# Two plain pairs of gate tiles, combinations in four steps, and scattered small loads in a two-layer encoder

## The chip, the cores and the metric

The kernel runs on one core of one Trainium2 chip. The metric is device time in microseconds (us) of one execution. The kernel before takes 3044.78 us (median of three runs, 3042.04 to 3044.88).

A core has a matrix engine (TensorE, PE in the profile), three engines for elementwise work (VectorE or DVE, ScalarE or ACT, GpSimd or POOL), and SyncE (SP), which here only starts transfers. TensorE reads its operands from on-chip memory and adds up in PSUM buffers, which another engine must empty. Each engine works through its own list of instructions in a fixed order; an instruction waits on semaphores for what others make, and what stands behind it on its engine waits with it. Transfers are started from SyncE's and GpSimd's lists.

## The reference

Two layers on 512 tokens of width 1024, in float32. Each layer is

```
h = h + 1/2 * SwiGLU_1(RMSNorm(h))
u = RMSNorm(h);  proj = u @ W_in
h = h + (sig(g_A)*o_A + sig(g_B)*o_B + sig(g_C)*o_C) @ W_out
h = h + 1/2 * SwiGLU_2(RMSNorm(h))
h = h + sigmoid(RMSNorm(h) @ W_pg) * (p[i] @ W_pp)
```

and the output is RMSNorm(h). A feed-forward is `(silu(x @ w_gate) * (x @ w_up)) @ w_down` with an inner width of 2816, that is 22 tiles of 128 ("gate tiles"; each has a gate and an up part). o_A is attention with low-rank queries and keys, o_B attention in a window of 128 with a logit for a sink, o_C the difference of two softmaxes, scaled by a learned lambda: `lam = exp(sum(lq1*lk1)) - exp(sum(lq2*lk2)) + lambda_init`. o_B and o_C add a bias that depends on the distance of two tokens and is looked up in a table of 32 buckets for 24 heads.

## The kernel before, in words

Every float32 value that TensorE uses is split in a high and a low part (`split` for activations, `Weights.part` for weights: a cast on ScalarE, names `whi`, `...h`, and a subtraction on VectorE or GpSimd, names `wlo`, `...l`). A product is then three matmuls (`mm3`): high by high, high by low, low by high. The activations stand transposed, 1024 features in 8 tiles of 128 x 512 tokens (`h`, in the trace `x`, `wo0h`, `wo1h`).

**A feed-forward** (`ffn`; ffn10 and ffn20 in layer 0, ffn11 and ffn21 in layer 1) works on the 22 gate tiles in 11 pairs. The first pair is *plain* (`plain_pair`): for each of its tiles f, 8 features by 3 matmuls of 512 columns for gate and as many for up. The norm's factor `rb` is multiplied in afterwards, so the matmuls can begin with the raw, gain-scaled `z` (`prep.z`). The other ten pairs are `Quad`s: the product of a 2 x 2 block of weights with a 2 x 2 block of activations (features in halves, tokens in halves A and B) is made with seven products instead of eight, each of 4 x 3 matmuls of 256 columns. The weights' sums are made by transfers that add (`accum_op`) and by `took`; the activations' combinations are made once for each feed-forward by `Combos.combine(k)` for k = 0 to 3: `t57k` for products 5 and 7, `t64k` for 6 and 4. The products of a pair come in the order 1, 2, then product 4 of the pair before, then 5, 6, 3, 7, each for gate (g) and up (u); V and R are the PSUM buffers of the results. So the first product that needs a combination is product 5 of the first `Quad`, after 48 matmuls of it. `gate_half` applies Silu and the norm factor (a multiply on GpSimd), `up_half` multiplies and splits to `a[f]`.

`DOWN_AFTER` says after which pair the down projection of a group of finished `a[f]` stands: group 0 (two tiles, 48 matmuls of 512 columns) after pair 1, group 1 (four tiles, 96 matmuls) after pair 3, and so on. Each of its eight results is added to `h[d]` by VectorE (L536).

**Order.** The code is written as one list of steps, with weight loads and splits prepared a fixed number of steps ahead (`load_upto`, `prepare`, `Weights`); a tile framework then places each engine's instructions by their dependencies and its own estimate of when they can run, so that instructions that wait for nothing late can move ahead of where the code has them. Whole weight chunks (512 KB) go through a ring of four buffers (`wraw`).

**Hooks** are small jobs that a feed-forward calls at a tile number f. In layer 0's first feed-forward: `load_tables` (f = 2, the bias table), `constants` (f = 4: the permutation matrix and, for each layer, the load of the four lambda vectors, two products, an exponential on ScalarE and the rest on VectorE), `bias_vectors` (f = 8: the table's lookups by matmul, their results `bvs` copied out and written to `bias_s` and `bias_d`, and then 24 transfers that spread each head's bias over 128 rows in `copies_s` and `copies_d`). The lambda loads and the bias copies are on GpSimd's queue.

Of the kernel before, what the change touches and what calls it, by code (L numbers as in the profile page):

```python
# [39 lines left out]
FFN_CHUNKS = 66  # L40

PAIRS = FT // 2
DOWN_AFTER = {1: 0, 3: 1, 5: 2, 7: 3}


def ffn_stream():

    res = []
    for p in range(PAIRS):
        res += [p] * 4  # L50
        if p in DOWN_AFTER:
            res += [None] * (2 if DOWN_AFTER[p] == 0 else 4)
    return res + [None] * 8


def whole(n):

    m = n % CHUNKS_PER_LAYER
    start = 0 if m < FFN_CHUNKS else CHUNKS_PER_LAYER - KT - FFN_CHUNKS
    return start <= m < start + FFN_CHUNKS and bool(ffn_stream()[m - start])  # L60


def lambda_init(i):
# [113 lines left out]
def encoder_kernel(ctx: ExitStack, tc: tile.TileContext, ins, out):  # L177
# [95 lines left out]
        return small[:, l * S_N + at:l * S_N + at + 1]  # L273

    def constants():
        nc.gpsimd.dma_start(perm, ins["perm"])
        for l in range(L):
            s = slice(l * NH, (l + 1) * NH)
            nc.vector.tensor_scalar(neg_sink[:, s], small[:, l * S_N + S_SINK:l * S_N + S_SINK + NH], -1.0, None, op0=ALU.mult)
            nc.vector.tensor_scalar(sub_gain[:, l:l + 1], col(l, S_SUB), 1.0 - lambda_init(l), None, op0=ALU.mult)  # L280
            lv = S(f"lamv{l}")
            nc.gpsimd.dma_start(lv[:, 0:256], ins["lam"][l])
            e = tiny(f"lam{l}")
            for j in range(2):
                pr = S(f"lamp{l}{j}")
                nc.vector.tensor_mul(pr[:, 0:64], lv[:, j * 128:j * 128 + 64], lv[:, j * 128 + 64:j * 128 + 128])
                nc.vector.tensor_reduce(e[:, j:j + 1], pr[:, 0:64], axis=AX.X, op=ALU.add)
            nc.scalar.activation(e[:, 2:4], e[:, 0:2], AF.Exp)

            nc.vector.tensor_scalar(e[:, 4:5], e[:, 3:4], -lambda_init(l), None, op0=ALU.add)  # L290
            nc.vector.tensor_sub(neg_lam[:, l:l + 1], e[:, 4:5], e[:, 2:3])
    tab, oh = [], []

    def load_tables():
        tab.append(S("tab"))
        nc.gpsimd.memset(tab[0][32:33, 0:24], 1.0)
        nc.gpsimd.dma_start(tab[0][0:32, 0:24], ins["rel_table"])
        for i in range(3):
            oh.append(S(f"oh{i}"))
            nc.gpsimd.dma_start(oh[i][0:33, :], ins["onehot"][:, i * 512:(i + 1) * 512])  # L300

    def bias_vectors():

        for i in range(3):
            ps = PS(f"bv{i}")
            heads = slice(0, NH) if i == 0 else slice(NH, NH + NHD)
            n = heads.stop - heads.start
            nc.tensor.matmul(ps[0:n, :], tab[0][0:33, heads], oh[i][0:33, :], start=True, stop=True)
            bv = S(f"bvs{i}")
            nc.vector.tensor_copy(bv[0:n, :], ps[0:n, :])  # L310
            if i == 0:
                nc.gpsimd.dma_start(bias_s, bv[0:n, :])
            else:
                nc.gpsimd.dma_start(bias_d[:, (i - 1) * 512:i * 512], bv[0:n, :])
        for vec, copies in ((bias_s, copies_s), (bias_d, copies_d)):
            for i in range(vec.shape[0]):
                nc.gpsimd.dma_start(copies[i], vec[i:i + 1, :].to_broadcast([P, vec.shape[1]]))

    def strip(vec, row, cols, tag, bufs, name, pool=sb):

# [188 lines left out]
    def ffn(l, tag, prep, after, hooks={}):  # L509
# [27 lines left out]
                if final:  # L537
                    after(d)

        def plain_pair():  # L540

            for f in range(2):
                pg, pu = PS(f"{name}g{f}"), PS(f"{name}u{f}")
                gate, up = ("cols", tag + "_w_gate", l, f), ("cols", tag + "_w_up", l, f)
                if f == 0:
                    together((pg, pu), W.get(gate, up), prep.z)
                    rstd()
                    prep.quarters()
                else:
                    run(proj(pg, W.get(gate), prep.z))  # L550
                    run(proj(pu, W.get(up), prep.z))
                g1, u1 = S(f"{name}g1_{f}"), S(f"{name}u1_{f}")
                nc.vector.tensor_mul(g1, pg, rb[0])
                nc.scalar.activation(g1, g1, AF.Silu)
                nc.vector.tensor_mul(u1, pu, rb[0])
                nc.vector.tensor_mul(u1, u1, g1)
                a[f] = split(u1, f"{name}a{f}")
                for k in (2 * f, 2 * f + 1):
                    prep.combine(k)

        def gate_half(q, n):

# [22 lines left out]
            steps.append(("product", (q, i), do))  # L585

        tail = []
        for p in range(1, PAIRS):
            G, U = [Quad(f"{name}{x}{p}", tag + "_w_" + w, p, prep) for x, w in (("g", "gate"), ("u", "up"))]
            for i in (1, 2):  # L590
                product(G, i)
# [14 lines left out]
            steps.insert(at + 2 + k, steps.pop())  # L606
        down(len(GROUPS) - 1, True)

        plain_pair()


        quads = []
# [33 lines left out]
        def prepare():  # L646
# [3 lines left out]
            load_upto(n + LOADS)  # L650
            if kind == "down":
                place = base[what]
                W.load(place + 1)
                hi, lo = W.tiles(stage)
                W.part(hi, lo, W.raw.pop(place))
                ready[n] = (hi, lo), state["tiles"]
                state["tiles"] += 1
                W.split = max(W.split, place + 1)
# [633 lines left out]
    for l in range(L):  # L1292
# [4 lines left out]
            18: lambda: p2.__setitem__(slice(0, 2), [split(t, f"p{l}_{k}") for k, t in enumerate(p2)]),  # L1297
        }
        if l == 0:
            hooks.update({2: load_tables, 4: constants, 8: bias_vectors})  # L1300
        ffn(l, "ffn1", prep, pm, hooks)
        close_stage()
        sums, outs = mix(l, pm, p2)
# [186 lines left out]
```

## Time and profile before

| | |
|---|---|
| median of 3 runs | 3044.78 us (3042.04 to 3044.88) |
| the profiled execution | 3043.61 us, span 3041.8 us |
| TensorE, VectorE, ScalarE, GpSimd busy | 96%, 71%, 55%, 37% of the span |
| mean granted clock of TensorE | 0.986 |
| matmuls in the trace | 17086 |

The view of waits reads "engine, what it was about to do, <- whom it waited for: us in total, times, longest". A row of the timeline or the chain begins with the start in us from the span's start, then the duration in us. The windows' table gives for a stretch the busy time of each engine with its instructions, the granted clock, the share of the DMA engines and GB/s. A group's row ends with the count, busy time and mean duration in ns, and the idle time before it with what ended most of it.

### The profile page before, as it was taken

What the parts mean: (1) busy time and instruction counts of PE and PEld (TensorE: products, weight loads), DVE (VectorE), ACT (ScalarE), POOL (GpSimd) and SP (SyncE); (2) the same over time, 40 slices, a digit from 0 to 9 for tenths busy, and PEclk for the clock granted to TensorE, in tenths of its full rate; (3) what the DMA queues carried; (4) which work ended last, traced back from release to release, by engine and by line L of the source; (5) the groups of instructions that cost most, each with busy time, mean ns of one, the idle gap of its engine ahead of it and who ended that gap; (6) DMA issues with size and microseconds to landing.
All of it is one profiled execution on the core that took longest, in us unless ns stands there. A gap on an engine that the chain in (4) does not pass through costs nothing.

```text
span 3041.8 us, 45943 instructions
## 1 busy us (share of the span) xinstructions
PE 2930.9 (96%) x17086; PEld 2566.1 (84%) x17086; DVE 2158.9 (71%) x3580; ACT 1666.8 (55%) x3201; POOL 1114.2 (37%) x1033
## 2 busy tenths in 40 slices
PE   7989999999999998999989999999999999899997
PEld 5879977888888888999879998788888878799996
DVE  7756767645788768777677777766467877676676
ACT  5434446655677755444454444566566777544453
POOL 2243213443445552333222331144444455432313
PEclk8999999999999999999989999999999999999999
DMA  6576342112222253656425553311212122655532
GB/s 209 145 226 165 95 161 70 56 63 76 80 72 69 77 185 98 172 154 165 140 70 160 146 153 128 117 63 56 70 68 81 62 79 82 191 142 142 151 96 83
DMA packets 116127, 351.21 MB, mean 115 GB/s; under 512 B 14222, under 2 KB 16270, under 8 KB 115904
## 3 DMA queue, kind: packets, MB, share of 16 engines
q1 hardware_dynamic: 78480, 261.39, 25.5%
q0 software_dynamic: 35120, 83.95, 12.6%
q8 instruction: 134, 2.20, 0.3%
q10 hardware_dynamic: 2304, 2.94, 0.3%
q14 instruction: 89, 0.73, 0.1%
HBM read 337.68 MB, written 18.94 MB: 117 GB/s over the span
## 4 chain that ended last, share of the span: by engine, by line
PE 76%; DVE 11%; ACT 5%; issue 4%; DMA 3%; POOL 1%; ACTq 0%; DVEq 0%; SPq 0%; POOLq 0%
PE ffn21d L218 4%; PE ffn11d L218 4%; PE ffn10d L218 4%; PE ffn20d L218 4%; PE ple L218 3%; DVE wlo L101 2%; PE m0ga L218 1%; PE m1ga L218 1%; PE m0gb L218 1%; PE m1gb L218 1%; PE m0vc L218 1%; PE m1vc L218 1%; PE m0qc L218 1%; PE m0kc L218 1%; PE m1qb L218 1%
## 5 line engine op out<-in xcount | busy, mean ns | idle before, releaser
L101 POOL TENSOR_TENSOR wlo<-wraw,whi 128x1024 fp32r<-128x1024 f32 x144 | 349.1, 2427 | 385.6 <-ACT whi L100 342.7
L100 ACT CAST whi<-wraw 128x1024 fp32r<-128x1024 f32 x296 | 310.5, 1051 | 212.5 <-issue 60.4
L101 DVE TENSOR_TENSOR wlo<-wraw,whi 128x1024 fp32r<-128x1024 f32 x152 | 189.9, 1252 | 93.3 <-ACT whi L100 92.9
L536 DVE SCALAR_TENSOR_TENSOR wo0h<-ffn11d,wo0h 128x512 f32<-128x512 f32 x48 | 32.9, 688 | 31.1 <-PE ffn11d L218 31.1
L536 DVE SCALAR_TENSOR_TENSOR wo1h<-ffn21d,wo1h 128x512 f32<-128x512 f32 x48 | 32.9, 688 | 29.2 <-PE ffn21d L218 29.2
L536 DVE SCALAR_TENSOR_TENSOR wo0h<-ffn20d,wo0h 128x512 f32<-128x512 f32 x48 | 32.9, 688 | 28.4 <-PE ffn20d L218 28.4
L536 DVE SCALAR_TENSOR_TENSOR x<-ffn10d,x 128x512 f32<-128x512 f32 x48 | 32.7, 687 | 25.4 <-PE ffn10d L218 25.4
L351 POOL TENSOR_TENSOR f_1sq<-f_1sq,f_1sq 128x512 f32<-128x512 f32 x14 | 21.5, 1533 | 42.9 <-ACT f_1sq L346 42.7
L894 ACT CAST m0kc<-m0kc 64x512 fp32r<-64x512 f32 x32 | 18.6, 582 | 18.5 <-PE m0kc L218 15.2
L894 ACT CAST m1kc<-m1kc 64x512 fp32r<-64x512 f32 x32 | 18.6, 582 | 18.5 <-PE m1kc L218 15.2
L847 DVE SCALAR_TENSOR_TENSOR m1qc<-m1qc,m1qc 64x512 fp32r<-64x512 f32 x16 | 11.0, 688 | 20.0 <-ACT m1qc L846 19.9
L847 DVE SCALAR_TENSOR_TENSOR m0qc<-m0qc,m0qc 64x512 fp32r<-64x512 f32 x16 | 11.0, 688 | 20.0 <-ACT m0qc L846 19.9
L846 ACT ACTIVATE m1qc<-m1qc 64x512 fp32r<-64x512 f32 x16 | 9.5, 594 | 21.4 <-PE m1qc L218 13.2
L846 ACT ACTIVATE m0qc<-m0qc 64x512 fp32r<-64x512 f32 x16 | 9.5, 593 | 21.4 <-PE m0qc L218 13.2
L1141 ACT ACT_TABLE_LOAD x16 | 20.5, 1283 | 0.3
L1313 POOL TENSOR_SCALAR out<-wo1h,small 128x512 f32<-128x512 f32 (+1 forms) x9 | 7.2, 795 | 33.0 <-DVE wo1h L1277 33.0
L351 POOL TENSOR_TENSOR pg0sq<-pg0sq,pg0sq 128x512 f32<-128x512 f32 x7 | 10.6, 1513 | 23.1 <-ACT pg0sq L346 23.1
L351 POOL TENSOR_TENSOR pg1sq<-pg1sq,pg1sq 128x512 f32<-128x512 f32 x7 | 10.6, 1512 | 23.1 <-ACT pg1sq L346 23.1
L915 DVE TENSOR_TENSOR m1vc<-m1vc,m1vc 128x256 fp32r<-128x256 f32 x16 | 6.4, 414 | 13.3 <-ACT m1vc L914 13.1
L915 DVE TENSOR_TENSOR m0vc<-m0vc,m0vc 128x256 fp32r<-128x256 f32 x16 | 6.4, 414 | 13.3 <-ACT m0vc L914 13.1
L1246 DVE SCALAR_TENSOR_TENSOR wo1h<-wo,wo1h 128x512 f32<-128x512 f32 x8 | 5.5, 685 | 12.9 <-DMA wo1h<-h_dram 12.9
L847 DVE SCALAR_TENSOR_TENSOR m1qb<-m1qb,m1qb 64x512 fp32r<-64x512 f32 x16 | 11.0, 688 | 4.8 <-ACT m1qb L846 4.5
(16244 smaller groups left out, 12882.1 us busy)
## 6 DMA issues: line engine op xcount, KB each, us to landing
wraw<-in_wall SPq DMA_DIRECT2D x296, 512.0 KB, 3.4
copies_s<-bias_s POOLq DMA_DIRECT2D x16, 256.0 KB, 8.6
copies_d<-bias_d POOLq DMA_DIRECT2D x8, 512.0 KB, 13.5
h_dram<-x POOLq DMA_DIRECT2D x8, 256.0 KB, 2.6
pp_dram<-m0ppt POOLq DMA_DIRECT2D x8, 256.0 KB, 4.3
wo0h<-h_dram POOLq DMA_DIRECT2D x8, 256.0 KB, 8.3
ple0p<-pp_dram POOLq DMA_DIRECT2D x8, 256.0 KB, 4.2
h_dram<-wo0h POOLq DMA_DIRECT2D x8, 256.0 KB, 2.6
```

The source lines that it names most:

```text
L100: self.nc.scalar.copy(hi, raw)
L101: self.lo_engine.tensor_tensor(lo, raw, hi.bitcast(F32), op=ALU.subtract)
L218: nc.tensor.matmul(ps, lhsT, rhs, start=start, stop=stop, skip_group_check=True)
L351: self.engine.tensor_tensor(self.acc, self.acc, sq, op=ALU.add)
L536: nc.vector.scalar_tensor_tensor(h[d], ps, 0.5, h[d], op0=ALU.mult, op1=ALU.add)
L846: nc.scalar.activation(qs[e][own], ps[own], AF.Copy, scale=-0.125)
L847: nc.vector.scalar_tensor_tensor(qs[e][other], ps[own], -0.125, qs[e][own].bitcast(F32), op0=ALU.mult, op1=ALU.subtract)
L894: nc.scalar.copy(ks[e][r], ps[own])
L915: nc.vector.tensor_sub(t[:, 256:512], ps, t[:, 0:256].bitcast(F32))
L1141: nc.scalar.activation(r, ss, AF.Sqrt, bias=eps, scale=1.0 / P)
L1246: nc.vector.scalar_tensor_tensor(h[d], sums[d], 0.5, h[d], op0=ALU.mult, op1=ALU.add)
L1313: nc.gpsimd.tensor_scalar(gained[d][:, c], h[d][:, c], small[:, L * S_N + d:L * S_N + d + 1], 1.0, op0=ALU.mult, op1=ALU.mult)
```

## The change

`PLAIN = 2`: the first two pairs (four gate tiles) of each feed-forward are computed plainly, each followed by one `combine` instead of two; the `Quad`s begin with pair 2. Down group 0 now stands right behind the plain pairs, ahead of the first `Quad`; its chunks may already have been split, and `prepare` then takes them from `W.parts`. The plain tiles call hooks too. The permutation matrix and the lambda vectors are loaded on SyncE's queue by `load_tables` (now called in the plain tiles); the rest of `constants` is called at f = 5. The 24 bias copies are taken out of `bias_vectors` and called four at a time at f = 11, 13, 15, 17, 19 and 20. Nothing is left out of the computation.

```diff
--- before.py
+++ after.py
@@ -40,6 +40,7 @@
 FFN_CHUNKS = 66
 
 PAIRS = FT // 2
+PLAIN = 2
 DOWN_AFTER = {1: 0, 3: 1, 5: 2, 7: 3}
 
 
@@ -57,7 +58,7 @@
 
     m = n % CHUNKS_PER_LAYER
     start = 0 if m < FFN_CHUNKS else CHUNKS_PER_LAYER - KT - FFN_CHUNKS
-    return start <= m < start + FFN_CHUNKS and bool(ffn_stream()[m - start])
+    return start <= m < start + FFN_CHUNKS and (ffn_stream()[m - start] or 0) >= PLAIN
 
 
 def lambda_init(i):
@@ -273,13 +274,11 @@
         return small[:, l * S_N + at:l * S_N + at + 1]
 
     def constants():
-        nc.gpsimd.dma_start(perm, ins["perm"])
         for l in range(L):
             s = slice(l * NH, (l + 1) * NH)
             nc.vector.tensor_scalar(neg_sink[:, s], small[:, l * S_N + S_SINK:l * S_N + S_SINK + NH], -1.0, None, op0=ALU.mult)
             nc.vector.tensor_scalar(sub_gain[:, l:l + 1], col(l, S_SUB), 1.0 - lambda_init(l), None, op0=ALU.mult)
-            lv = S(f"lamv{l}")
-            nc.gpsimd.dma_start(lv[:, 0:256], ins["lam"][l])
+            lv = lams[l]
             e = tiny(f"lam{l}")
             for j in range(2):
                 pr = S(f"lamp{l}{j}")
@@ -289,9 +288,13 @@
 
             nc.vector.tensor_scalar(e[:, 4:5], e[:, 3:4], -lambda_init(l), None, op0=ALU.add)
             nc.vector.tensor_sub(neg_lam[:, l:l + 1], e[:, 4:5], e[:, 2:3])
-    tab, oh = [], []
+    tab, oh, lams = [], [], []
 
     def load_tables():
+        nc.sync.dma_start(perm, ins["perm"])
+        for l in range(L):
+            lams.append(S(f"lamv{l}"))
+            nc.sync.dma_start(lams[l][:, 0:256], ins["lam"][l])
         tab.append(S("tab"))
         nc.gpsimd.memset(tab[0][32:33, 0:24], 1.0)
         nc.gpsimd.dma_start(tab[0][0:32, 0:24], ins["rel_table"])
@@ -312,9 +315,12 @@
                 nc.gpsimd.dma_start(bias_s, bv[0:n, :])
             else:
                 nc.gpsimd.dma_start(bias_d[:, (i - 1) * 512:i * 512], bv[0:n, :])
-        for vec, copies in ((bias_s, copies_s), (bias_d, copies_d)):
-            for i in range(vec.shape[0]):
-                nc.gpsimd.dma_start(copies[i], vec[i:i + 1, :].to_broadcast([P, vec.shape[1]]))
+
+    def bias_copies(n):
+
+        for i in range(4 * n, 4 * n + 4):
+            vec, copies, i = (bias_s, copies_s, i) if i < NH else (bias_d, copies_d, i - NH)
+            nc.gpsimd.dma_start(copies[i], vec[i:i + 1, :].to_broadcast([P, vec.shape[1]]))
 
     def strip(vec, row, cols, tag, bufs, name, pool=sb):
 
@@ -537,9 +543,9 @@
                 if final:
                     after(d)
 
-        def plain_pair():
-
-            for f in range(2):
+        def plain_pairs():
+
+            for f in range(2 * PLAIN):
                 pg, pu = PS(f"{name}g{f}"), PS(f"{name}u{f}")
                 gate, up = ("cols", tag + "_w_gate", l, f), ("cols", tag + "_w_up", l, f)
                 if f == 0:
@@ -555,8 +561,9 @@
                 nc.vector.tensor_mul(u1, pu, rb[0])
                 nc.vector.tensor_mul(u1, u1, g1)
                 a[f] = split(u1, f"{name}a{f}")
-                for k in (2 * f, 2 * f + 1):
-                    prep.combine(k)
+                prep.combine(f)
+                if f in hooks:
+                    hooks[f]()
 
         def gate_half(q, n):
 
@@ -585,7 +592,8 @@
             steps.append(("product", (q, i), do))
 
         tail = []
-        for p in range(1, PAIRS):
+        down(DOWN_AFTER[PLAIN - 1])
+        for p in range(PLAIN, PAIRS):
             G, U = [Quad(f"{name}{x}{p}", tag + "_w_" + w, p, prep) for x, w in (("g", "gate"), ("u", "up"))]
             for i in (1, 2):
                 product(G, i)
@@ -606,7 +614,7 @@
             steps.insert(at + 2 + k, steps.pop())
         down(len(GROUPS) - 1, True)
 
-        plain_pair()
+        plain_pairs()
 
 
         quads = []
@@ -650,9 +658,12 @@
             load_upto(n + LOADS)
             if kind == "down":
                 place = base[what]
-                W.load(place + 1)
-                hi, lo = W.tiles(stage)
-                W.part(hi, lo, W.raw.pop(place))
+                if place in W.parts:
+                    hi, lo = W.parts.pop(place)
+                else:
+                    W.load(place + 1)
+                    hi, lo = W.tiles(stage)
+                    W.part(hi, lo, W.raw.pop(place))
                 ready[n] = (hi, lo), state["tiles"]
                 state["tiles"] += 1
                 W.split = max(W.split, place + 1)
@@ -1297,7 +1308,8 @@
             18: lambda: p2.__setitem__(slice(0, 2), [split(t, f"p{l}_{k}") for k, t in enumerate(p2)]),
         }
         if l == 0:
-            hooks.update({2: load_tables, 4: constants, 8: bias_vectors})
+            hooks.update({2: load_tables, 5: constants, 8: bias_vectors})
+            hooks.update({11 + 2 * n - n // 5: lambda n=n: bias_copies(n) for n in range(6)})
         ffn(l, "ffn1", prep, pm, hooks)
         close_stage()
         sums, outs = mix(l, pm, p2)
```

The list of TensorE has 17005 rows before and 16717 now. Three places in the order follow, each first as it was and then as it is.

GpSimd in layer 0's first feed-forward, from the bias vectors (`bias_s`, `bias_d`) on; `ffn10g4t` is the multiply of pair 4's gate by the norm factor, its second row that of the pair's second half; `ffn10g6y` to `ffn10u7z` are weight loads that add:

```order
L570 TENSOR_TENSOR ffn10g4t_1445<-ffn10g4t_1445,f_0r 128x512
L312 DMA bias_s<-bvs_1663 16x512
L314 DMA bias_d<-bvs_1668 8x512
L314 DMA bias_d<-bvs_1673 8x512
L469 DMA ffn10g6y<-in_wall 128x512
L317 DMA copies_s<-bias_s 128x512 x16
L317 DMA copies_d<-bias_d 128x1024 x8
L469 DMA ffn10u6y<-in_wall 128x512
L570 TENSOR_TENSOR ffn10g4t_1446<-ffn10g4t_1446,f_0r 128x512
L470 DMA ffn10g7z<-in_wall 128x512
L470 DMA ffn10u7z<-in_wall 128x512
```

```order
L315 DMA bias_s<-bvs_1541 16x512
L317 DMA bias_d<-bvs_1546 8x512
L317 DMA bias_d<-bvs_1551 8x512
L475 DMA ffn10g6y<-in_wall 128x512
L475 DMA ffn10u6y<-in_wall 128x512
L323 DMA copies_s<-bias_s 128x512 x6
L577 TENSOR_TENSOR ffn10g4t_1324<-ffn10g4t_1324,f_0r 128x512
L323 DMA copies_s<-bias_s 128x512 x5
L476 DMA ffn10g7z<-in_wall 128x512
L476 DMA ffn10u7z<-in_wall 128x512
L323 DMA copies_s<-bias_s 128x512 x5
L323 DMA copies_d<-bias_d 128x1024
```

Before, all 24 copies stand ahead of the second half's multiply. Now six stand ahead of it, and the others between the next loads and the multiply of pair 5 and behind it (the row after these is `copies_d` once, then `ffn10g5t`).

ScalarE at the program's start; `z0h` to `z7h` are the high parts of the activations, `whi` a weight's high part:

```order
L100 CAST whi_124<-wraw_80 128x1024
L392 ACTIVATE f_0z0h<-x_70,small 128x512
L100 CAST whi_128<-wraw_82 128x1024
L392 ACTIVATE f_0z1h<-x_71,small 128x512
L100 CAST whi_187<-wraw_185 128x1024
L392 ACTIVATE f_0z2h<-x_72,small 128x512
L392 ACTIVATE f_0z3h<-x_73,small 128x512
L392 ACTIVATE f_0z4h<-x_74,small 128x512
```

```order
L101 CAST whi_124<-wraw_80 128x1024
L398 ACTIVATE f_0z0h<-x_70,small 128x512
L101 CAST whi_128<-wraw_82 128x1024
L398 ACTIVATE f_0z1h<-x_71,small 128x512
L101 CAST whi_187<-wraw_185 128x1024
L398 ACTIVATE f_0z2h<-x_72,small 128x512
L101 CAST whi_626<-ffn10g2x 128x512
L398 ACTIVATE f_0z3h<-x_73,small 128x512
```

The cast of the first `Quad`'s weights (`ffn10g2x`) now stands ahead of `z3h`. VectorE has the weights' low part ahead of `z3l` in the same way.

VectorE at the start of layer 1's first feed-forward, where the last combinations are made (`f_1t572`, `f_1t573` and their partners `t642`, `t643`):

```order
L437 TENSOR_TENSOR f_1t_15649<-f_1zf_15647 128x256
L439 SCALAR_TENSOR_TENSOR f_1t_15649<-wo0h_11241,small,f_1zf_15647 128x256
L438 SCALAR_TENSOR_TENSOR f_1t_15650<-wo0h_11241,nsmall,f_1t_15649 128x256
L440 SCALAR_TENSOR_TENSOR f_1t_15650<-wo0h_11241,nsmall,f_1t_15650 128x256
L230 TENSOR_TENSOR f_1t572l<-f_1t_15649,f_1t572h 128x512
L230 TENSOR_TENSOR f_1t642l<-f_1t_15650,f_1t642h 128x512
L437 TENSOR_TENSOR f_1t_15665<-f_1zf_15663 128x256
L439 SCALAR_TENSOR_TENSOR f_1t_15665<-wo0h_11243,small,f_1zf_15663 128x256
L438 SCALAR_TENSOR_TENSOR f_1t_15666<-wo0h_11243,nsmall,f_1t_15665 128x256
L440 SCALAR_TENSOR_TENSOR f_1t_15666<-wo0h_11243,nsmall,f_1t_15666 128x256
L230 TENSOR_TENSOR f_1t573l<-f_1t_15665,f_1t573h 128x512
L230 TENSOR_TENSOR f_1t643l<-f_1t_15666,f_1t643h 128x512
```

```order
L443 TENSOR_TENSOR f_1t_15491<-f_1zf_15489 128x256
L445 SCALAR_TENSOR_TENSOR f_1t_15491<-wo0h_11119,small,f_1zf_15489 128x256
L444 SCALAR_TENSOR_TENSOR f_1t_15492<-wo0h_11119,nsmall,f_1t_15491 128x256
L102 TENSOR_TENSOR wlo_15622<-ffn11g2x,whi_15621 128x512
L446 SCALAR_TENSOR_TENSOR f_1t_15492<-wo0h_11119,nsmall,f_1t_15492 128x256
L231 TENSOR_TENSOR f_1t572l<-f_1t_15491,f_1t572h 128x512
L542 SCALAR_TENSOR_TENSOR wo0h_11107<-ffn11d_0_15626,wo0h_11107 128x512
L231 TENSOR_TENSOR f_1t642l<-f_1t_15492,f_1t642h 128x512
L559 TENSOR_TENSOR ffn11g_3_15563<-ffn11g_15505,f_1r 128x512
L561 TENSOR_TENSOR ffn11u_3_15564<-ffn11u_15506,f_1r 128x512
L542 SCALAR_TENSOR_TENSOR wo0h_11109<-ffn11d_1_15634,wo0h_11109 128x512
L562 TENSOR_TENSOR ffn11u_3_15564<-ffn11u_3_15564,ffn11g_3_15563 128x512
```

Before, combinations 2 and 3 stand back to back behind the evictions of plain tile 1, with matmuls of the first `Quad` already listed. Now combination 2 stands behind plain tile 2, and evictions of down group 0 (`ffn11d`) and of plain tile 3 come between it and combination 3.

## The prediction

> **What bounds the kernel now.** I read the page's busy shares, its slices and its chain first, then the steady part of one feed-forward, then the four places where TensorE stands still. All times are of the one profiled execution, 3043.61 us with a span of 3041.8.
>
> ```profile
> PE 2930.9 (96%) x17086; PEld 2566.1 (84%) x17086; DVE 2158.9 (71%) x3580; ACT 1666.8 (55%) x3201; POOL 1114.2 (37%) x1033
> PE 76%; DVE 11%; ACT 5%; issue 4%; DMA 3%; POOL 1%; ACTq 0%; DVEq 0%; SPq 0%; POOLq 0%
> ```
>
> TensorE is busy for 96% of the span and is 76% of the chain, so the kernel is matmul bound; what is left is 111 us in which TensorE is idle, and stretches at a lower clock, below. The eleven hundredths of the chain on VectorE say who is late when TensorE waits.
>
> The pace without a stall, from the chain and from the table of windows (us, then busy time of each engine, clock, DMA share, GB/s):
>
> ```profile
> 1231.82 21.79 PE ffn20d L218 x96
> 1255.04 1.44 PE ffn20u4R L218 x12
> 1293.92 21.79 PE ffn20d L218 x96
> 1232.00:1294.00 62.00, 62.00 (x434) 58.23 (x433) 43.96 (x69) 27.77 (x53) 18.70 (x17) 1.00 0.56 153
> ```
>
> A matmul of 512 columns takes 21.79/96 = 0.227 us, one of 256 columns 1.44/12 = 0.120. From one down group to the next lie 62.10 us: two pairs with quarter products, 168 matmuls or 20.16 us each, and the group. TensorE never waits there; VectorE has 18 us of every 62 free, so it is slack in the middle of a feed-forward and not at its start:
>
> ```profile
> 35.12:69.50 34.38, 22.56 (x146) 20.91 (x145) 28.75 (x52) 21.29 (x37) 3.56 (x5) 0.75 0.48 117
> 1150.42:1179.54 29.12, 20.70 (x145) 19.65 (x144) 24.16 (x45) 17.59 (x32) 2.11 (x3) 0.82 0.39 109
> 1553.25:1587.59 34.34, 23.22 (x146) 21.57 (x144) 27.71 (x50) 20.39 (x35) 2.15 (x3) 0.75 0.33 92
> 2645.83:2674.81 28.98, 20.56 (x146) 19.50 (x145) 24.16 (x45) 17.60 (x32) 2.11 (x3) 0.82 0.39 109
> PE ffn11g1V L218 <- ACT f_1t572h L229: 5.2, 1, 5.2
> PE ffn20g1V L218 <- ACT f_0t572h L229: 5.5, 1, 5.5
> 1565.00:1581.00 16.00, 9.48 (x38) 8.45 (x39) 12.20 (x22) 8.10 (x15) 1.79 (x2) 0.50 0.43 102
> ```
>
> Each of the four windows goes from the first matmul of the first quarter-product pair to the first matmul of the down group: 144 matmuls of 256 columns, 144 x 0.12 = 17.28 us when nothing is late. They take 34.38, 29.12, 34.34 and 28.98, so 17.1, 11.8, 17.1 and 11.7 us are lost, 57.7 together. The wait named is for the combined operands (t57), the longest 5.2 and 5.5 us, and after it the clock is 0.50 for 16 us, which doubles a matmul. VectorE is busy 24 to 29 us in these windows, more than the 17.28 that TensorE needs: the operands are late because VectorE has the splits of quarter-product weights and all four combinations at once.
>
> **The change, part by part.** *Second plain pair (gain 57.7, price 6.5).* Plain tiles 2 and 3 need no combined operand, and a combination now stands behind each of four plain tiles instead of two behind each of two. A pair done plainly is 96 matmuls of 512 columns, 21.79 us, for 20.16: 1.63 us dearer, 6.5 over four feed-forwards. So much is sure.
>
> What of the 57.7 goes? The combinations' VectorE rows, a weight split, a down group's eviction, and a split that meets a GpSimd operation:
>
> ```profile
> 1558.99 0.42 DVE L437 TENSOR_TENSOR f_1t<-f_1zf 128x256 f32<-128x256 f32 x1
> 1559.32 0.48 DVE L439 SCALAR_TENSOR_TENSOR f_1t<-wo0h,small,f_1zf 128x256 f32<-128x256 f32 x1
> 1561.11 0.68 DVE L230 TENSOR_TENSOR f_1t570l<-f_1t,f_1t570h 128x512 fp32r<-128x512 f32 x1
> 1587.29 1.78 DVE L101 TENSOR_TENSOR wlo<-ffn11u2x,whi 128x512 fp32r<-128x512 f32 x1
> L101 DVE TENSOR_TENSOR wlo<-wraw,whi 128x1024 fp32r<-128x1024 f32 x152 | 189.9, 1252 | 93.3 <-ACT whi L100 92.9
> L536 DVE SCALAR_TENSOR_TENSOR wo0h<-ffn11d,wo0h 128x512 f32<-128x512 f32 x48 | 32.9, 688 | 31.1 <-PE ffn11d L218 31.1
> ```
>
> Starts lie some 0.1 us nearer than the durations, so a combination (a 0.42, three of 0.48, two splits of 0.68) holds VectorE about 2.7 us. A plain tile (two weight splits 2.5, four evictions and splits 2.4, a combination 2.7) is about 8 us on VectorE against 10.9 on TensorE: three combinations are hidden under plain matmuls. The fourth is not. Behind the last plain matmul VectorE still has that tile's eviction (2.4), the combination (2.7), eight down evictions (8 x 0.6), and some nine half splits (9 x 0.6) and two sums of weights (0.8) that the changed order puts ahead: 16 us, and 2 more where splits meet GpSimd (1.78 for 0.68). The order also has the first down eviction ahead of plain tile 3's own, so VectorE first waits for six matmuls of the down group, 1.4 us, if it is idle by then. TensorE has 48 matmuls of the down group (10.9) and two products (5.8) before the first combined operand: 16.7. So 0 to 4 us per start are late; I take 2, the middle, because the combination stands ahead of most splits: 8 in all.
>
> *Lambda loads (gain 4.9).* The chain, the wait, and ScalarE's timeline:
>
> ```profile
> 110.30 4.79 DMA lamv<-in_lam
> 116.28 2.11 PE ffn10g3R L218 x12
> 118.39 2.51 PE ffn10u3R L218 x12
> PE ffn10g3R L218 <- ACT ffn10g3t L499: 3.2, 1, 3.2
> 112.69 1.28 ACT L288 ACT_TABLE_LOAD   x1
> 115.77 0.20 ACT L288 ACTIVATE lam<-lam 128x2 f32<-128x2 f32 x1 [1.79 <-DVE lam L287]
> ```
>
> ScalarE loads the table of the second layer's exponential and stands until 115.77 for a transfer on GpSimd's queue; the copies of pair 3 behind it hold TensorE for 3.2 us, and 24 matmuls then take 4.63 for 2.88. Both loads now lie on SyncE's queue long before the constants, and both exponentials stand together: 3.2 + 1.7 = 4.9 gone. The two table loads that stay (1.28 each; one from and one to the other function) are covered by the quarter products of the pair before; uncovered they would cost 2.6.
>
> *Bias copies (gain 11.8).* The chain, the wait, GpSimd's and VectorE's timelines, and the DMA's window:
>
> ```profile
> 126.65 21.79 PE ffn10d L218 x96
> 228.53 1.43 PE ffn10g6R L218 x12
> 207.99 2.56 PE ffn10g5V L218 x12
> 210.55 2.51 PE ffn10u5V L218 x12
> PE ffn10d L218 <- ACT ffn10a9h L229: 9.6, 1, 9.6
> 177.67 4.20 POOL L317 DMA_DIRECT2D copies_s<-bias_s  x8 [0.74 <-DMA bias_s<-bvs]
> 200.79 0.52 POOL L317 DMA_DIRECT2D copies_d<-bias_d  x1 [0.93 <-DMA copies_s<-bias_s]
> 204.11 1.59 POOL L570 TENSOR_TENSOR ffn10g4t<-ffn10g4t,f_0r 128x512 f32<-128x512 f32 x1
> 205.74 0.43 DVE L577 SCALAR_TENSOR_TENSOR ffn10u4t<-ffn10u4t,ffn10g4t 128x256 f32<-128x256 f32 x1 [10.92 <-POOL ffn10g4t L570]
> 201.00:213.00 12.00, 5.80 (x26) 5.76 (x27) 3.84 (x8) 1.16 (x3) 4.26 (x5) 0.57 1.03 344
> ```
>
> Down group 1 ends at 148.44 and group 2 at 228.53: 80.1 us for 62.1. Of the 18 lost, 9.6 is the wait for a9, whose multiply stands on GpSimd behind 24 copies, the last at 200.79; VectorE stood 10.92 us behind it. The 24 matmuls after it take 5.07 for 2.88. These 11.8 can go; the other 6, the bias vectors' own matmuls and splits, stay. The changed order puts six copies ahead of that multiply, 6 x 0.52 = 3.1 us of issue: it is ready before it is needed. The next pair's multiply gets eleven copies and two weight loads ahead; by the old wait per copy (24 from 177.67 to 201.3, near 1 us each) it may be 2 to 7 us late, with VectorE held behind it while PSUM buffers let TensorE run on. Price 0 to 5, taken 0 beyond what the 8 above hold.
>
> *Start-up (price 2).* In layer 0's first feed-forward ScalarE and VectorE now have the split of g2x ahead of z3. Its load takes the old place of g1x:
>
> ```profile
> 9.58 0.43 SPq L467 DMA_DIRECT2D ffn10g1x<-in_wall  x1
> ffn10g1x<-in_wall SPq DMA_DIRECT2D x1, 512.0 KB, 6.8
> 16.56 0.39 PE L218 MATMUL ffn10g<-f_0z3h,whi 128*128 128x512 f32 x1
> ```
>
> The two issue rows give 16.4 for the landing; perm, now ahead of it on SyncE's queue, adds one issue of 0.4, and the two lambda loads come later and ahead of nothing that is wanted soon, so they cost nothing. Then a cast (0.6), z3h and z3l (0.7 each) follow, 18.4 for z3l where TensorE wants it at 17.0: 1 to 3 us, taken 2; 5 if the load is later.
>
> **Two rules of the Trainium skill against this.** "TensorE: Matmul & The Clock Gate", section "Back-to-back issue gap", gives an isolated matmul N/2.4 + 2.5 ns, hence 215.8 ns at 512 columns and 109.2 at 256; the pair would be 2.4 us dearer and the gain 3 us smaller (an estimate). The rows say 227 and 120, and they decide. The same page, "What's actually happening", has the half clock come after an idle window of about 3.4 us; the start-up gap of 2 us would by that rule stay without one. Here 3.2 us of idle did bring slow matmuls.
>
> **The sum.** 57.7 - 6.5 + 4.9 + 11.8 - 2 - 8 = 57.9 us. 3043.6 - 57.9 = 2985.7; the median of the runs shown lies 1.2 above the profiled one, so 2987.
>
> **The rivals.** *A: VectorE stays late at the new join.* At 18 us of work against 16.7 it is over the edge already. Speaking for it: any idle over 3 us so far was followed by the half clock, and GpSimd's additions lie close. Against: the second half of the splits may run after the combination. With 5 us per start in place of 2: 2999. *B: the copies are not spread.* The hooks name six pairs, but the order shows all 24 within two pairs, so the DMA queues saturate as before (344 GB/s at a share of 1.03), and the a9 or a11 multiply is still behind. Without the 11.8: 2999 as well. *C, the other side: plain chunks bind.* A plain tile needs two whole chunks; if a load, a cast and a split came only after the chunk before was used, each would expose them:
>
> ```profile
> wraw<-in_wall SPq DMA_DIRECT2D x296, 512.0 KB, 3.4
> L100 ACT CAST whi<-wraw 128x1024 fp32r<-128x1024 f32 x296 | 310.5, 1051 | 212.5 <-issue 60.4
> ```
>
> 3.4 + 1.05 + 1.25 = 5.7 us on 16 more chunks is 91 us, 3078; it decides the sign from 3.6 us a chunk. Against it: the 296 whole chunks elsewhere run with TensorE at 96%.
>
> **How the numbers follow.** The forecast has 0.70 (2975, with no late combination, no gap at the start and 2 us of smaller waits gone, to 2993, A halfway), A 0.14, B 0.11, C 0.03, and 0.02 that gains and late work cancel. The range 2970 to 3008 holds the forecast, A and B, most of both together at 3008, and 5 us below the forecast's own end for slow-clock matmuls that I count as staying. About 0.2%, 6 us, is what a measurement tells from no change; that gives faster 0.95, same 0.02, slower 0.03.
>
> **What would show it.** Right: the four windows become a plain tile pair and a down group with waits for t57 below 2 us, no clock of 0.50 in the slices behind; ScalarE's two lambda exponentials adjacent with no wait for a transfer; down groups 1 and 2 about 68 us apart. Wrong: a wait for t573 of 4 us or more followed by slow matmuls (A); a wait for a9 or a11 above 5 us (B); waits for whi or wlo of plain chunks (C); a wait for z3 above 4 us at the start.

## The result, and the profile after

The changed kernel takes 2992.73 us (median of four runs, 2988.8 to 2994.54) against 3044.83 for the kernel before: a ratio of 0.9826, with a 95% interval of 0.9809 to 0.9843. It is 52 us faster, where 58 were forecast, and lies inside the range. The same kernel, run again later, had a median of 3000.62 against 3046.91, a ratio of 0.9847 (0.9833 to 0.9860). The profiled execution of the change took 2994.54 us, with a span of 2992.8 against 3041.8, so the trace explains 49.0 us.

The busy shares and the chain by engine, from the page of the change:

```profile
PE 2918.2 (98%) x16798; PEld 2544.4 (85%) x16798; DVE 2139.2 (71%) x3516; ACT 1639.8 (55%) x3135; POOL 1074.0 (36%) x998
PE 80%; DVE 9%; ACT 4%; issue 3%; DMA 2%; POOL 1%; SPq 0%; ACTq 0%; DVEq 0%; POOLq 0%
```

TensorE is idle for 74.6 us where it was idle for 110.9, and the mean granted clock rose from 0.986 to 0.996. Layer 0's first feed-forward, from the chain of waits:

```profile
58.75 10.88 PE ffn10d L219 x48
69.63 1.43 PE ffn10g2R L219 x12
...
107.06 21.79 PE ffn10d L219 x96
...
173.43 21.79 PE ffn10d L219 x96
```

Down group 0 begins the moment the plain matmuls end, and from its end at 69.63 to the next group at 107.06 stand 37.4 us of matmuls at 0.12 us each without a gap: no wait for a combined operand is left. The groups that ended 80.1 us apart (148.44 and 228.53) now end at 128.85 and 195.22, 66.4 us apart. What TensorE waits for now, the longest of the rows that the view of waits did not have before or has longer:

```profile
PE ffn21u L219 <- DVE wlo L102: 3.4, 1, 3.4
PE m1ckvss L377 <- DVE m1ckvsq L357: 3.0, 1, 3.0
...
PE ffn20u L219 <- DVE wlo L102: 2.4, 1, 2.4
PE m0C7s L219 <- DVE m0C7m L1112: 2.3, 2, 1.9
PE wo L219 <- ACT m1mg7h L230: 2.0, 1, 2.0
PE wo L219 <- ACT m0mg7h L230: 2.0, 1, 2.0
PE ffn11u2V L219 <- DVE wlo L102: 1.9, 1, 1.9
PE ffn21g L219 <- DVE wlo L102: 1.7, 1, 1.7
```

The waits for the low parts of plain weights (`wlo` for ffn21, ffn20) are at the start of both second feed-forwards; the row of ffn11u2V is a wait for the low part of a quarter-product weight at the start of ffn11. The other four are in the two attention stages (m0, m1 and their output projection `wo`), which the diff does not touch.

To see where the time went, take from both timelines the start of the same matmul and subtract. The lead of the change, in us:

| first matmul of | before | change | lead |
|---|---|---|---|
| ffn10, pair 3 (ahead of the lambda stall) | 101.44 | 86.74 | 14.7 |
| ffn10, pair 4 (behind down group 1) | 148.28 | 128.69 | 19.6 |
| ffn10, pair 6 (behind down group 2) | 228.36 | 195.05 | 33.3 |
| ffn20 | 1126.67 | 1098.66 | 28.0 |
| ffn20, pair 4 | 1253.44 | 1215.91 | 37.5 |
| ffn11 | 1529.54 | 1491.91 | 37.6 |
| ffn11, pair 4 | 1661.48 | 1609.71 | 51.8 |
| ffn21 | 2622.45 | 2575.67 | 46.8 |
| ffn21, pair 4 | 2747.86 | 2697.46 | 50.4 |
| end of the span | 3041.8 | 2992.8 | 49.0 |

By these marks the feed-forwards won 60.7 us. Then 5.3 and 5.0 were lost between the last mark of each first feed-forward and the start of the second, mostly in the attention stages, and the last 1.4 behind the first matmul of the final norm (lead 50.4 there).

### The profile page after: what moved, and what is told of

Read it like the earlier page. It is cut to its first block, busy times and chain, and to the rows that moved or that the text cites. A ratio compares the mean times of both kernels' runs of the same rounds, so it can differ in the third digit from the quotient of the medians.

```text
span 2992.8 us, 45125 instructions
## 1 busy us (share of the span) xinstructions
PE 2918.2 (98%) x16798; PEld 2544.4 (85%) x16798; DVE 2139.2 (71%) x3516; ACT 1639.8 (55%) x3135; POOL 1074.0 (36%) x998
## 4 chain that ended last, share of the span: by engine, by line
PE 80%; DVE 9%; ACT 4%; issue 3%; DMA 2%; POOL 1%; SPq 0%; ACTq 0%; DVEq 0%; POOLq 0%
PE ffn20d L219 4%; PE ffn10d L219 4%; PE ffn21d L219 4%; PE ffn11d L219 4%; PE ple L219 3%; DVE wlo L102 2%; PE m1ga L219 2%; PE m0ga L219 1%; PE m0gb L219 1%; PE m1gb L219 1%; PE m1vc L219 1%; PE m0vc L219 1%; PE wo L219 1%; PE m1qa L219 1%; PE m1qc L219 1%
## 5 line engine op out<-in xcount | busy, mean ns | idle before, releaser
L101 ACT CAST whi<-wraw 128x1024 fp32r<-128x1024 f32 x312 | 326.9, 1051 | 219.5 <-issue 59.3
L102 DVE TENSOR_TENSOR wlo<-wraw,whi 128x1024 fp32r<-128x1024 f32 x168 | 213.2, 1272 | 75.3 <-ACT whi L101 74.6
L857 ACT ACTIVATE m0qc<-m0qc 64x512 fp32r<-64x512 f32 x16 | 9.5, 593 | 21.4 <-PE m0qc L219 13.5
L858 DVE SCALAR_TENSOR_TENSOR m0qb<-m0qb,m0qb 64x512 fp32r<-64x512 f32 x16 | 11.0, 688 | 5.1 <-ACT m0qb L857 4.7
```

Of the source, the lines that this page charges most:

```text
L101: self.nc.scalar.copy(hi, raw)
L102: self.lo_engine.tensor_tensor(lo, raw, hi.bitcast(F32), op=ALU.subtract)
L857: nc.scalar.activation(qs[e][own], ps[own], AF.Copy, scale=-0.125)
L858: nc.vector.scalar_tensor_tensor(qs[e][other], ps[own], -0.125, qs[e][own].bitcast(F32), op0=ALU.mult, op1=ALU.subtract)
```

## The experiments

**The small loads alone.** The kernel before, with the change's lines for the small loads and nothing else, among them:

```diff
-            nc.gpsimd.dma_start(lv[:, 0:256], ins["lam"][l])
+            nc.sync.dma_start(lams[l][:, 0:256], ins["lam"][l])
...
+            hooks.update({11 + 2 * n - n // 5: lambda n=n: bias_copies(n) for n in range(6)})
```

> One plain pair with two combinations behind each tile, as before; only the small loads as changed: perm and lambda on SyncE's queue, the copies in six hooks. My theory (the parts add): the lambda stall of 4.9 and the removable 11.8 of the bias stall go, nothing else; 3044.8 - 16.7 = 3028, the four starts keep their 29 to 34 us and their waits for t57, and the mixes stay as before. Rival (the small loads were covered by other lateness, or the copies clump again): 3038 to 3045, with a wait for a9 above 5 us. Second rival (the reordered first layer moves more than these stalls): below 3022.

Measured: 3030.27 us against 3043.0, ratio 0.9953 (0.9938 to 0.9968). Its lead is 5.2 us at pair 4 and 17.6 at pair 6, so the lambda part is 4.9 and the copies 12.4. At the end 15.7 of it are left: 2.7 went at layer 1's output projection, in waits for low parts of its weights, though TensorE's order there is that of the kernel before. The four starts keep their waits for t57, as this row of its waits shows:

```profile
PE ffn20g1V L218 <- ACT f_0t572h L229: 5.5, 1, 5.5
```

**The plain pairs alone.** The change, with perm, lambda loads and copies put back:

```diff
-                nc.gpsimd.dma_start(bias_d[:, (i - 1) * 512:i * 512], bv[0:n, :])
-
-    def bias_copies(n):
...
+        for vec, copies in ((bias_s, copies_s), (bias_d, copies_d)):
+            for i in range(vec.shape[0]):
+                nc.gpsimd.dma_start(copies[i], vec[i:i + 1, :].to_broadcast([P, vec.shape[1]]))
```

> Two plain pairs and four combination steps as changed; perm, lambda loads and the 24 copies as before. My theory (the parts add): 2992.7 + 16.7 = 3009, with the 3.2 us wait for lambda and the 9.6 us wait for a9 back in the first feed-forward, and no wait for t57. It also tells whose the new losses are: if the waits for plain weights at the second feed-forwards and the early m1ckvss stay here, they belong to the plain pairs. Rival (parts overlap, the bias stall is smaller with the order shifted): 2995 to 3003.

Measured: 3013.08 us, ratio 0.9894 (0.9878 to 0.9910). Its waits:

```profile
PE ffn10d L219 <- DVE ffn10u4t L580: 9.4, 1, 9.4
PE m1ckvss L372 <- DVE m1ckvsq L352: 3.0, 1, 3.0
PE ffn10g3R L219 <- ACT ffn10g3t L500: 2.9, 1, 2.9
...
PE ffn21u L219 <- DVE wlo L102: 2.1, 1, 2.1
PE wo L219 <- ACT m0mg7h L230: 2.0, 1, 2.0
```

The two old stalls are back, and of the change's new waits most are here, while the kernel with the small loads alone has none of those at m1ckvss, at mg7 or for plain weights at ffn21, and 0.6 us at ffn20u, where the kernel before has 0.8: they belong to the plain pairs. Whether the parts add is not settled by the totals. By the profiled spans 3041.8 - 3026.1 = 15.7 and 3041.8 - 3007.0 = 34.8 make 50.5, and the change has 49.0; by the medians they make 42.7 of 52. The runs of one kernel spread over some 6 us, and the two profiles are of the fastest run of their kernels while that of the change is of its slowest. Stage by stage the parts agree with the change within 1.3 us: lambda 4.9 and copies 12.4 alone, 4.9 and 13.7 in the change; ffn10 to pair 3, ffn20 and ffn11 win 14.7, 9.4 and 14.1 with the pairs alone, 14.7, 9.5 and 14.1 in the change. Only ffn21 differs more, 6.2 against 3.6.

**Each small load put back alone.** First all 24 copies behind the bias vectors, then perm and lambda on GpSimd's queue, in the change:

> As changed, but all 24 copies follow the bias vectors at once. My theory (GpSimd's queue: the multiply of pair 4's second half stands behind the copies): down group 2 is 10 to 14 us later, the wait for a9 of 8 to 10 us is back, 3003 to 3007. Rival (the DMA queues are full either way and the order of the copies does not matter): within 4 us of the change.

> As changed, but perm and the lambda vectors load on GpSimd's queue when the constants are made. My theory: the wait of 3 us for the copies of pair 3 and the slow matmuls behind it are back, 4 to 6 us slower, 2997 to 2999. Rival (with more time between the loads and the exponential, hook 5 and not pair 2, the load comes in time): within 3 us of the change, both exponentials adjacent.

Measured: 3009.93 us (ratio 0.9883, 0.9868 to 0.9897) and 2997.87 (0.9850, 0.9828 to 0.9873). With the copies together the lead at pair 6 is 19.2 in place of 33.3, 14.1 us lost, with this wait, first row; with the lambda loads back the lead at pair 4 is 16.6 in place of 19.6, 3.0 lost, second row (each from its own kernel's waits). The first median lies above the 3003 to 3007 expected, though the loss in the stage is as expected. In the second the wait is back, but not the slow matmuls behind it (third row: the windows' table of that kernel, clock 1.00):

```profile
PE ffn10d L219 <- DVE ffn10u4t L582: 10.8, 1, 10.8
```

```profile
PE ffn10g3R L219 <- ACT ffn10g3t L503: 2.8, 1, 2.8
```

```profile
101.00:104.00 3.00, 2.82 (x23) 2.82 (x24) 2.41 (x7) 2.41 (x8) 0.00 (x0) 1.00 0.63 195
```

So it is the place of the copies in GpSimd's list that counts. In the change that list reads, from GpSimd's timeline:

```profile
159.20 3.19 POOL L323 DMA_DIRECT2D copies_s<-bias_s  x6 [0.72 <-DMA bias_s<-bvs]
162.41 1.31 POOL L577 TENSOR_TENSOR ffn10g4t<-ffn10g4t,f_0r 128x512 f32<-128x512 f32 x1
...
179.10 1.55 POOL L577 TENSOR_TENSOR ffn10g5t<-ffn10g5t,f_0r 128x512 f32<-128x512 f32 x1
```

The copies are not spread over six pairs (the last leaves at 188.42), but only six of them, 3.2 us, stand ahead of the multiply that the down group needs. The next multiply, behind eleven more copies, stops nobody: no wait for a11 is in the list.

**When the combinations are made.** In the change, all four behind plain tile 3, or two each behind tiles 0 and 1:

```diff
-                prep.combine(f)
+                for k in range(4) if f == 3 else ():
+                    prep.combine(k)
```

> As changed, but all four combinations stand behind plain tile 3. My theory (what counts is VectorE's work between the last plain matmul and product 5): three more combinations, 8 us, join some 16 us of work against 16.7 us of TensorE, so t57 is 6 to 10 us late at each start and half-clock matmuls follow; 25 to 50 us slower than the change, 3018 to 3043. Rival (the second plain pair and the down group give enough time by themselves, VectorE's list was never full): within 6 us of the change, 2987 to 2999.

```diff
-                prep.combine(f)
+                for k in (2 * f, 2 * f + 1) if f < 2 else ():
+                    prep.combine(k)
```

> As changed, but combinations 0, 1 stand behind plain tile 0 and 2, 3 behind tile 1, two steps as before. My theory: a plain tile's 8 us on VectorE become 10.8 against 10.9 on TensorE, still covered, and the last combination is out of the way at product 5; the time is that of the change within 4 us, 2989 to 2997. Rival (the four steps are needed: VectorE falls behind in tiles 0 and 1 and the plain matmuls wait): 3000 or more, with waits for plain weights' low parts in every feed-forward. Second rival (the fourth combination still costs the change something at the join): 4 to 8 us faster, 2985 to 2989.

Measured: 3020.94 us when last (ratio 0.9919, 0.9899 to 0.9939), 2990.47 when early (0.9825, 0.9805 to 0.9844). Waits of the kernel with the combinations last:

```profile
PE ffn11u2V L219 <- DVE wo0h L542: 3.6, 1, 3.6
...
PE ffn10g2V L219 <- ACT f_0t573h L230: 2.9, 1, 2.9
```

It loses 7.4, 2.9, 8.3 and 3.1 us at the four starts, 22 together, where 6 to 10 at each were expected: the time fell into the range, but only the first feed-forwards lost that much. There VectorE's list between the last plain matmul and product 5 is full, as the theory has it, and what is late in layer 1 is not a combination but the down evictions behind them (`wo0h`). By the medians it is 28 us slower than the change; where the other 6 go was not traced. Early, it is the change's time. So of "two pairs, operands made in four steps" the second pair is what gains; four steps are as good as two. The second pair and the down group that now stands ahead of the first `Quad` were not run apart, so how much of the cover each gives is not shown.

**The casts ahead of the activations.** ScalarE in the change at the end of layer 1's attention, from its timeline:

```profile
2570.92 0.62 ACT L101 CAST whi<-ffn21u2y 128x512 fp32r<-128x512 f32 x1 [7.76 <-DMA ffn21u2y<-in_wall]
...
2571.98 0.71 ACT L398 ACTIVATE f_1z3h<-wo1h,small 128x512 fp32r<-128x512 f32 x1
```

The cast of a weight of the first quarter-product pair, wanted 60 us later, was put ahead of z3, and ScalarE stood 7.8 us for its transfer with z3 to z7 and the casts of plain weights behind it. The tied kernel makes those casts wait for z7:

```diff
                     state["half"] = W.tiles(stage), state["tiles"]
+                    if state["tied"] < TIED:
+                        nc.scalar.copy(state["half"][0][0][:, 0:1024:512], prep.z[KT - 1][0].bitcast(F32)[:, 0:2])
+                        state["tied"] += 1
```

> As changed, but the first three weight tiles of each feed-forward's first quarter-product pair get two columns copied from the last activation tile z7 ahead of their own cast, so ScalarE cannot have those casts ahead of the activations. My theory (the casts of ffn21u2y and ffn10g2x, put ahead of z3, make ScalarE wait for a transfer, 7.8 us in ffn21, and the plain weights behind it come late): the waits of 3.4 and 1.7 us at ffn21 and of 1.0 at ffn10 go, 5 to 8 us faster than the change, 2985 to 2988; ffn20, where no such cast stands ahead, keeps its 2.4. Rival (the plain chunks themselves arrive late, the two loads for each tile are the bound): 2990 to 2996, with the wait for the plain weights' low part at ffn21 still 3 us or more.

Measured: 2985.05 us, ratio 0.9797 (0.9782 to 0.9812). The plain stage of ffn21, to its first down matmul, first in the change and then in the tied kernel, from the windows' table:

```profile
2575.60:2627.20 51.60, 46.51 (x196) 37.38 (x195) 40.50 (x47) 25.18 (x34) 10.48 (x8) 0.97 0.43 122
```

```profile
2570.30:2614.80 44.50, 44.50 (x196) 36.47 (x196) 35.64 (x44) 23.55 (x32) 7.17 (x6) 1.00 0.42 127
```

196 matmuls take 44.5 us without a gap where the change took 51.6. The plain chunks are therefore in time by themselves. ffn10 wins 2.5 us by the same cause. My expectation for ffn20 was wrong: it wins 2.8 us too. There the cast of g2x stands ahead of z0, but ScalarE did not stand for it (no idle time before it, at 1074.53), so why the tie helps there is not shown. The spans are 12.8 us apart, the slowest run of the change against the fastest of the tied kernel; the medians are 7.7 apart, on two chips. The size at ffn21 is in part chance: in the repeat of the change, below, ScalarE stands 7.0 us at the same cast, and the stage is only 3.0 us longer than in the tied kernel.

**The phase of the PSUM buffers.** With two plain pairs the order of TensorE in the attention stages differs from before in more than 200 rows, with one pair in none. The piece that costs most, TensorE before and in the change:

```profile
1940.86 1.02 PE L371 MATMUL m1cqss<-m1cqsq,ones 128*128 128x512 f32 x2
1944.92 1.07 PE L371 MATMUL m1ckvss<-m1ckvsq,ones 128*128 128x512 f32 x2
```

```profile
1890.42 1.02 PE L377 MATMUL m1cqss<-m1cqsq,ones 128*128 128x512 f32 x2
1894.40 1.13 PE L377 MATMUL m1ckvss<-m1ckvsq,ones 128*128 128x512 f32 x2 [2.96 <-DVE m1ckvsq L357]
```

Before, 14 matmuls of the gate m1ga stood between these two and hid the wait. Now the second stands directly behind the first, and m1ga behind both. PSUM buffers are dealt out in a cycle of eight turns (`CYCLE`), counted through the program, and two more plain tiles take four more turns in each feed-forward. One line puts the counter right:

```diff
         plain_pairs()
+        turn[0] += 4 * (PLAIN - 1)
```

With it the attention stages' order on TensorE is that of the kernel before, row by row. I ran it on the tied kernel, on the change, and beside them the change itself once more:

> As the tied kernel, and behind the plain pairs the counter that deals out PSUM buffers in a cycle of eight is put forward by four, so that every stage behind takes its buffers at the phase it had before the change; the order of the mixes' instructions on TensorE is then that of the kernel before. My theory (the second plain pair takes four more buffers, this shifts the phase, and with it m1ckvss and the output projection's matmuls were put elsewhere): the 3.0 us wait for m1ckvsq and the two waits of 2.0 for mg7 go, with the slow matmuls behind them; 8 to 11 us faster than tied, 2974 to 2978. Rival (these waits come with the earlier end of the feed-forward, not with the order): within 3 us of tied, 2982 to 2988, the same waits.

> The change with the phase put right and no tie. My theory (the two causes are separate): 8 to 11 us faster than the change, 2981 to 2985, both mixes as long as in the kernel before, and the waits for plain weights' low parts at ffn20 and ffn21 still there, 2 to 5 us together since one cast, u2y, now stands behind z4 and not behind z2. Rival (the order of the mix's end was the cause of those waits too): 2976 or less.

> The change itself once more, beside the two kernels above on one chip: 2989 to 2995 by its first four runs; the profile shows which of its waits repeat. By my theory those with a cause in the order do (m1ckvsq 3.0, mg7 2.0 twice, the low parts at ffn21 5.1 together), the 2.3 us at m0C7 need not.

Measured on one chip: 2979.57 us (ratio 0.9781, 0.9767 to 0.9794), 2988.56 (0.9809, 0.9796 to 0.9823) and 3000.62 (0.9847, 0.9833 to 0.9860). The waits for m1ckvsq and for mg7 are gone in both and are back in the third. From m1cqss to the first matmul of m1va the change loses 2.9 us of lead, the change again 2.9, the tied kernel 1.2, the two corrected ones nothing. Putting the phase right is worth 12 us on the change by medians and 8.4 by spans, against 8 to 11 expected. The waits for low parts stay there without the tie, 2.6 at ffn21u and 0.7 at ffn20u, within the 2 to 5 expected; the first attention stage stays 2.2 us longer than before, with a wait of 1.8 for a low part of its output weights. Both times that I named for the change were missed: 2988.56 for 2981 to 2985, and 3000.62 for 2989 to 2995. The kernel before was only 2 us slower on this chip, so that does not explain the 8 us of the repeat. The repeat has both waits of 2 us at m0C7s and m1C7s, and of the low parts at ffn21 only 2.1 us came back where I expected 5.1: that size does not repeat. On the tied kernel the gain came out at 5.5 us by medians of two chips and 2.3 by spans, between my theory and the rival: its profile has the two waits at C7s that the tied one lacks (below). The kernel with both edits is 21 us faster than the change on the same chip and the fastest of all here.

## Why the prediction was right

The time and the sign were right, and the terms about the removed stalls held. By the leads of the table, and in the last column by those of the change's repeat:

| term | forecast | measured | repeat |
|---|---|---|---|
| start of ffn10, to pair 3 | 17.1 - 1.6 - 2 - 2 = 11.5 | 14.6 | 14.5 |
| ffn20 | 11.8 - 1.6 - 2 = 8.2 | 9.5 | 10.7 |
| ffn11 | 17.1 - 1.6 - 2 = 13.5 | 14.1 | 14.2 |
| ffn21 | 11.7 - 1.6 - 2 = 8.1 | 3.6 | 7.6 |
| lambda | 4.9 | 4.9 | 4.9 |
| bias copies | 11.8 | 13.7 | 13.7 |
| attention stages and end | 0 | -11.7 | -16.8 |

The total came close in part by luck: the starts and the copies gave more than was forecast, and the attention stages, forecast at nothing, took that and more.

**Second plain pair.** That t57 came late because VectorE was full at the start, and that the second pair would cover it, is shown by the two kernels with the combinations moved. The price of a plain pair held: 5.44/24 = 0.227 us and 1.44/12 = 0.12 are unchanged.

**The residual at the join** was mis-sized: 2 us per start were taken, and no wait for t57 is left at all. Only ffn11 waits 1.9 us for the low part of a weight of product 2. Rival A did not happen; with 8 us more of VectorE's work at that place (combinations last) a wait for t573 of 2.9 us came at ffn10 and one of 3.6 for the down evictions at ffn11, so the edge that the estimate saw is there, a little further off.

**Lambda loads and bias copies** went as forecast and for the reasons given, by the kernels that put each back. Of lambda's 4.9 only the 3.2 of the wait is sure, though: put back alone it cost 3.0, without slow matmuls. Rival B named something true, that the copies leave within two pairs, but not its consequence: what stands ahead of pair 4's multiply decides, not how far the copies are spread.

**Start-up.** The wait for z3 was 1.0 us and the stage 2.5 us longer than with the cast moved away; 2 was taken. The step that failed is that this was costed at layer 0's start alone. A cast of the same kind, u2y, stands ahead of z3 at ffn21; the tied kernel was 7.1 us faster there than the change and 3.0 faster than its repeat. At ffn20 it was faster by 2.8 and 1.5. These look like rival C (waits for plain weights), but the tied kernel shows that the loads themselves are in time.

**What was not foreseen** is the attention stages. The prediction priced them at nothing without a row for it: that they are not in the diff was taken for unchanged. Of the 11.7 us, 6.1 were lost where the order had moved (2.9 at m1ckvss, 2.2 and 1.0 at the two output projections with their waits for mg7), which the corrected phase shows; 2.5 at m0C7s, the chance part, which the repeat has in both layers; 1.4 at the end; and most of the rest in the last pairs of ffn10 and ffn11, which nothing here tried to change. The shortfall of ffn21 and these stages took 16 us; better starts and copies gave 7 back.

Of the two rules of the Trainium skill that were weighed, the one in "TensorE: Matmul & The Clock Gate", section "Back-to-back issue gap", did not give the price here: the pace stayed at 227 and 120 ns. In the change no slow clock followed the 2.0 us wait for m0mg7h (first row), and one followed the 3.0 us wait for m1ckvsq (second row):

```profile
1075.00:1077.00 2.00, 2.00 (x10) 1.53 (x9) 0.95 (x2) 0.15 (x1) 2.00 (x5) 1.00 0.83 257
...
1895.00:1898.00 3.00, 3.00 (x10) 2.19 (x9) 3.00 (x2) 0.69 (x1) 0.00 (x0) 0.63 0.60 203
```

The length of the wait does not decide it. Behind the same two waits it is the other way round in the repeat of the change (first row, behind m0mg7h) and in the tied kernel (second row, behind m1ckvsq):

```profile
1077.00:1079.00 2.00, 2.00 (x6) 1.61 (x5) 0.00 (x0) 0.00 (x0) 1.36 (x3) 0.50 0.99 245
```

```profile
1889.00:1892.00 3.00, 3.00 (x12) 2.16 (x13) 3.00 (x1) 0.69 (x1) 0.00 (x0) 1.00 0.73 266
```

So a wait of 2 to 3 us sometimes brings a few microseconds at the half clock and sometimes none, and a price such as lambda's 3.2 + 1.7 holds only its first part for certain. It fits that m1ckvss cost the tied kernel 1.2 us and the change 2.9. The idle window of about 3.4 us that the Trainium skill names in "TensorE: Matmul & The Clock Gate", section "What's actually happening", is no limit here below which a wait is safe: 2.0 us sufficed in the repeat.

## What to carry to other kernels

An in-order engine pays for whatever its list holds ahead of the urgent work, however early that other work may be: look in the order for transfers and casts wanted much later that stand in front of what is wanted now (24 copies, one cast of u2y). A change that takes another number of buffers from a shared ring can alter the order of stages that it does not touch, so compare the order of the whole program and price each piece that moved. Cover for late operands is measured in the late engine's own list, from the last work that must wait to the first use.

## What was not expected of the hardware

The wait at m0C7s or m1C7s comes and goes between executions: m1C7s waits 2.0 us in the repeat of the change and 0.5 in the change. VectorE and GpSimd at that place, before (first) and in the change:

```profile
899.17 1.83 DVE L1113 SCALAR_TENSOR_TENSOR m0C6p<-m0C6p,m0C6r,m0C6p 128x512 f32<-128x512 f32 x2 [0.30 <-POOL m0C6p L920]
...
900.30 5.31 POOL L101 TENSOR_TENSOR wlo<-wraw,whi 128x1024 fp32r<-128x1024 f32 x2 [0.50 <-ACT whi L100]
```

```profile
866.16 4.07 DVE L1124 SCALAR_TENSOR_TENSOR m0C6p<-m0C6p,m0C6r,m0C6p 128x512 f32<-128x512 f32 x2 [0.31 <-POOL m0C6p L931]
...
867.28 5.21 POOL L102 TENSOR_TENSOR wlo<-wraw,whi 128x1024 fp32r<-128x1024 f32 x2 [0.49 <-ACT whi L101]
```

GpSimd's split begins 1.13 us behind VectorE's first operation in the one and 1.12 in the other, and yet VectorE's two operations take 1.83 us before and 4.07 in the change, 2.2 more. All that follows is later by that much. The Trainium skill, "SBUF — State Buffer", section "Terms", has the two engines share a pair of ports under a lock held for a whole instruction, so that the loser stands still; 2.2 us more against a split of 2.4 agrees with that. A wait of 1.9 or 2.0 us at C7s stands in 9 of 24 such places (two in each of the twelve profiles of these kernels), and costs 2.3 to 2.5 us of lead each. In these nine VectorE's second operation takes 2.97 us and GpSimd's split 2.40; in the other fifteen they take 0.74 and 2.97, so one of the two loses each time, and only VectorE's loss is seen by TensorE. It may be part of why runs of one kernel spread by 6 us. What decides it was not tried.
